# First block's score maps: q and k split in place, and the two maps of a job run on the two halves of the array's rows in turns

## The chip, the core and the metric

The kernel runs on one core of a Trainium2 chip. The metric is the device time of one launch in microseconds. The core has a matrix engine (TensorE, PE in the profile; its weight loads are shown as PEld), a vector engine (DVE), a scalar engine (ACT), GpSimd (POOL), and a sync engine (SP) that issues most DMAs. PE writes its results into PSUM banks; DVE and ACT read them from there.

## The reference, cut to what matters

Two transformer blocks run one after the other on 256 rows of 2048 numbers. The first has two layers; each is a product with `w_in`, a differential attention, two side branches and a product with `w_out`. The change touches the scores of that attention alone. There are 8 heads, and each head has two maps `i` of 64 numbers:

```python
def _diff_attn(qb, k_all, v_all, lam):
    s = jnp.einsum('bqhid,bkhid->bhiqk', qb.astype(jnp.float32) * ATTN_SCALE, k_all.astype(jnp.float32))
    p = jax.nn.softmax(s, axis=-1)
    a = p[:, :, 0] - lam * p[:, :, 1]
    return jnp.einsum('bhqk,bkhe->bqhe', a.astype(v_all.dtype), v_all)
```

In layer 0 the 256 context rows attend to themselves (256 keys) and the 256 rows of x attend to context and x (512 keys). In layer 1 only the rows of x attend (512 keys).

## The kernel before, in words

Every large product is made of three matmuls in the one-pass type `fp32r`: each operand is split into a rounded part (hi) and the rest (lo), and hi·hi, hi·lo and lo·hi are summed in a PSUM bank (`mm3`, L247 to L249; where the two parts of an activation lie side by side, two matmuls do it, L267 and L269). The weights come in blocks of 512 KB by DMA (L177, L182). ACT makes hi of a block (L185) and DVE makes lo (L186).

The attention of the first block is a generator (`attention`) that is stepped beside the weight products: `bg_step` takes one step of it after every chunk of weights (in layer 1 after every second chunk). It works in **jobs**: a job is 128 query rows of one head. Layer 0 has 4 jobs a head, two with 256 keys and two with 512; layer 1 has 2 jobs a head with 512 keys. With 8 heads that makes 48 jobs, 16 with 256 keys and 32 with 512. Attention runs four heads at a time, so there are four groups of jobs in the span.

For each head `parts(h)` prepares the operands. A head's `q` and `k` are tiles of 128 partitions: map 0 lies on partitions 0 to 63 and map 1 on 64 to 127. For each map it builds a stacked `q` (hi in the map's own half, lo in the other half; L649 on ACT, L650 on DVE), a `k` with its hi in both halves (L651 and L652 on ACT), and the lo of `k` in the map's half (L653 on POOL). All of these work on 64 partitions.

For each job `scores` then runs, map after map, two matmuls into one PSUM bank: L663 over all 128 rows (it gives hi·hi and lo·hi at once) and L664 over the 64 rows of the map's half (hi of q times lo of k). DVE takes the row maximum (L665), ACT the exponential (L672), DVE normalises and subtracts (L676 to L679); two steps later PE transposes (L686), and at the end of a head multiplies with v (L696) and transposes again (L712).

The PSUM tiles of the attention (`aux`) come from a ring of three banks. A job takes two of them for its maps, and a third goes to the transposes of an older job. The `qs` tiles come from a ring of ten.

The Python order is not quite the order on the engines. A scheduler of the framework places instructions by its own cost model, within the data dependencies. So it can put weight matmuls between the maps of a job: in 18 of the 48 jobs of before, weight matmuls or transposes stand between the two maps. Each engine then runs its own list in order.

The side work that the rows name: L404 and L406 on DVE are products with the modulation weights, spread over the first half of the span; L416 and L434 sum their result over the partitions with a 32-column operand per stream, in plain fp32 (each is recorded as two passes), and L423 transposes it on 64 rows; L339 and L340 are the helper `split` (hi on ACT, lo on DVE).

## Time and profile before

| what | value |
|---|---|
| median of 3 runs | 2966.14 us (2965.07 to 2972.32) |
| the profiled execution: its own time | 2966.39 us |
| its span | 2964.5 us |
| PE, DVE, ACT, POOL busy, share of the span | 98%, 67%, 41%, 10% |
| granted TensorE clock, mean | 0.991 of 2.4 GHz |

A page of the profile gives busy times over the whole span; rows by stretch give them for a part of it, timeline rows give the start of each instruction and its recorded duration. Matmuls are pipelined, so the duration of one overlaps the next. What a matmul costs the engine is read from the distance between its start and the start of the next one, called pitch here.

### The profile page before, as it was taken

To read this page: it belongs to the slowest core of one execution; us is meant where nothing else is said; L and a number is where in the kernel's file an instruction comes from. 1 tells how busy PE (TensorE), PEld (TensorE's weight loads), DVE (VectorE), ACT (ScalarE), POOL (GpSimd) and SP (SyncE) were. 2 spreads that over 40 slices of the span, in tenths; PEclk is the share of its full clock that TensorE was granted. 3 is DMA by queue.
4 is the path that set the end of the run, shared out by engine and by line. 5 is a ranking of instruction groups with operands and counts; after the bars stand their busy time and mean duration, and the time that the engine had idled before them with its cause. 6 is when DMAs were issued, how large, how long until landed. Compare 5 with 4: busy or idle time off the path is not lost.

```text
span 2964.5 us, 38716 instructions
## 1 busy us (share of the span) xinstructions
PE 2899.2 (98%) x14802; PEld 2382.4 (80%) x14802; DVE 1978.0 (67%) x2890; ACT 1213.7 (41%) x1750; POOL 296.9 (10%) x319
## 2 busy tenths in 40 slices
PE   8999999999999999999988999999999999999998
PEld 5677778678779787878876888888888888888887
DVE  3779987887985649568665565766655556555564
ACT  3123433432311436246434454544444434444444
POOL 0001001101100411011210000000101102011011
PEclk9999999999999999999998999999999999999999
DMA  8764445346664336545754545455565655555555
GB/s 308 265 204 136 130 154 177 128 142 211 215 196 164 121 116 199 166 137 184 243 176 135 185 144 198 157 187 190 185 197 166 195 190 184 199 185 192 191 187 169
DMA packets 156435, 533.86 MB, mean 180 GB/s; under 512 B 17860, under 2 KB 21196, under 8 KB 156248
## 3 DMA queue, kind: packets, MB, share of 16 engines
q1 hardware_dynamic: 148656, 510.79, 52.2%
q0 software_dynamic: 5632, 18.36, 2.0%
q10 hardware_dynamic: 1960, 2.22, 0.3%
q8 instruction: 116, 1.90, 0.3%
q14 instruction: 71, 0.58, 0.1%
HBM read 527.07 MB, written 4.23 MB: 179 GB/s over the span
## 4 chain that ended last, share of the span: by engine, by line
PE 71%; issue 5%; DVE 2%; DMA 1%; ACT 1%; POOL 0%; ACTq 0%; POOLq 0%; DVEq 0%
PE acc L267 22%; PE acc L269 11%; PE acc L247 11%; PE acc L249 11%; PE acc L248 11%; PE aux L696 1%; PE aux L664 1%; PE aux L663 0%; DVE lo L186 0%; PE aux L686 0%; PE aux L1083 0%; ACT hi L185 0%; DVE p L952 0%; DMA raw<-in_w_in_dram 0%; POOL small L123 0%
## 5 line engine op out<-in xcount | busy, mean ns | idle before, releaser
L186 DVE TENSOR_TENSOR lo<-raw,hi 128x1024 fp32r<-128x1024 f32 x766 | 942.1, 1233 | 683.9 <-ACT hi L185 677.9
L185 ACT CAST hi<-raw 128x1024 fp32r<-128x1024 f32 x769 | 805.4, 1050 | 1355.1 <-PE acc L249 472.3
L267 PE MATMUL acc<-act,hi 128*128 128x512 f32 x2960 | 1052.1, 400 | 0.6 <-DVE qs L306 0.6
L269 PE MATMUL acc<-act,lo 128*128 128x256 f32 x2960 | 830.7, 281 | 4.6 <-DVE lo L186 4.6
L267 PEld LDWEIGHTS acc<-act,hi 128*128 128x128 f32 x2960 | 555.3, 188 | 139.8 <-issue 3.5
L247 PE MATMUL acc<-hi,act 128*128 128x512 f32 (+1 forms) x1568 | 582.7, 372 | 1.5 <-ACT act L339 1.3
L248 PE MATMUL acc<-lo,act 128*128 128x512 f32 (+1 forms) x1568 | 578.9, 369 | 0.2 <-DVE lo L186 0.2
L249 PE MATMUL acc<-hi,act 128*128 128x512 f32 (+1 forms) x1568 | 578.4, 369 | 0.5 <-DVE act L340 0.5
L269 PEld LDWEIGHTS acc<-act,lo 128*128 128x128 f32 x2960 | 558.3, 189 | 8.2 <-DVE lo L186 6.3
L406 DVE SCALAR_TENSOR_TENSOR ma<-mod,cc,ma 128x512 f32<-128x512 f32 x480 | 344.1, 756 | 25.2 <-DMA mod<-in_w_mod_dram 23.4
L247 PE MATMUL acc<-act,hi 128*128 128x512 f32 x896 | 359.2, 401 | 0.5 <-DVE p L764 0.5
L249 PE MATMUL acc<-act,lo 128*128 128x512 f32 x896 | 351.7, 393 | 0.0
L248 PE MATMUL acc<-act,hi 128*128 128x512 f32 x896 | 351.6, 392 | 0.0
L247 PEld LDWEIGHTS acc<-hi,act 128*128 128x128 f32 x1568 | 296.4, 189 | 54.4 <-issue 3.2
L248 PEld LDWEIGHTS acc<-lo,act 128*128 128x128 f32 x1568 | 296.7, 189 | 50.1 <-DVE lo L186 1.4
L249 PEld LDWEIGHTS acc<-hi,act 128*128 128x128 f32 x1568 | 296.4, 189 | 49.9 <-DVE act L340 1.1
L247 PEld LDWEIGHTS acc<-act,hi 128*128 128x128 f32 x896 | 168.8, 188 | 55.3 <-issue 9.4
L249 PEld LDWEIGHTS acc<-act,lo 128*128 128x128 f32 x896 | 168.8, 188 | 39.3 <-issue 3.6
L248 PEld LDWEIGHTS acc<-act,hi 128*128 128x128 f32 x896 | 168.9, 189 | 35.6 <-issue 3.0
L315 DVE TENSOR_REDUCE tmp<-acc 128x256 f32<-128x512 f32 x169 | 112.9, 684 | 52.2 <-PE acc L269 52.2
L1190 POOL TENSOR_TENSOR tmp<-tmp 128x256 f32<-128x256 f32 x64 | 69.7, 1089 | 566.8 <-ACT tmp L1189 539.4
L340 DVE TENSOR_TENSOR act<-tmp,act 128x256 fp32r<-128x256 f32 (+1 forms) x96 | 58.3, 614 | 45.7 <-ACT act L339 45.7
(214 smaller groups left out, 1792.5 us busy)
## 6 DMA issues: line engine op xcount, KB each, us to landing
raw<-in_w_in_dram SPq DMA_DIRECT2D x384, 512.0 KB, 3.4
mod<-in_w_mod_dram SPq DMA_DIRECT2D x158, 512.0 KB, 3.9
raw<-in_w_up_dram SPq DMA_DIRECT2D x128, 512.0 KB, 4.4
raw<-in_w_down_dram SPq DMA_DIRECT2D x128, 512.0 KB, 4.3
raw<-in_w_out_dram SPq DMA_DIRECT2D x96, 512.0 KB, 4.3
mod<-in_w_mod_dram SPq DMA_DIRECT2D x68, 256.0 KB, 5.0
raw<-in_w_proj_a_dram SPq DMA_DIRECT2D x16, 512.0 KB, 3.8
raw<-in_w_proj_b_dram SPq DMA_DIRECT2D x16, 512.0 KB, 4.3
```

Source lines behind the costliest of these rows:

```text
L185: S.copy(hi, raw)
L186: (fn or V).tensor_sub(lo, raw, hi)
L247: mm(ps, lh, rh, start=start, stop=False)
L248: mm(ps, lh, rl, start=False, stop=False)
L249: mm(ps, ll, rh, start=False, stop=stop)
L267: mm(p[:w, :].rearrange("p (a t) -> p a t", a=2), hi[:, kk, c:c + w], act.both(k0 + kk, tok), start=start, stop=False)
L269: mm(p[:w, :ntok], lo[:, kk, c:c + w], ah[:, tok], start=False, stop=stop)
L315: V.reduce_sum(t, ps[0], axis=AX.X)
L340: V.tensor_sub(lo, src, h)
L406: V.scalar_tensor_tensor(st[s], raw[:, kk, :], cc2[:, k, s:s + 1], st[s], op0=ALU.mult, op1=ALU.add)
L664: mm(p[:, :nk], qi[r, q0:q0 + P], kl[r, 0:nk], start=False, stop=True)
L1190: G.tensor_mul(t, t, t)
```

## The change

It does four things, all in the attention of the first block:

- `parts` no longer builds stacked copies. It calls the helper `split` on the whole `q` tile and on the whole `k` tile of a head: one ACT cast and one DVE subtraction each, over 128 partitions. It takes 4 `qs` tiles a head where there were 5. POOL has no part in it any more.
- `scores` takes both PSUM banks of a job first.
- Each map's scores are three matmuls over the 64 rows of its own half (hi·hi, hi·lo, lo·hi) where there were one over 128 rows and one over 64. A job has six matmuls where it had four.
- The six are written in turns: map 0 on the lower half of the rows into its bank, map 1 on the upper half into its own, three times.

```diff
         def parts(h):
-            q, k = qt_[h], kt_[h]
-            nq, nk = q.shape[-1], k.shape[-1]
-            r = lambda n: qs_tile()[:, :n].bitcast(F32R)
-            L, H = slice(0, 64), slice(64, P)
-            a0, a1, b0, b1, kl = r(nq), r(nq), r(nk), r(nk), r(nk)
-            for t, b, s, d in ((a0, b0, L, H), (a1, b1, H, L)):
-                S.copy(t[s], q[s])
-                V.tensor_sub(t[d], q[s], t[s])
-                S.copy(b[s], k[s])
-                S.copy(b[d], k[s])
-                G.tensor_sub(kl[s], k[s], b[s])
-            return (a0, b0, kl, L), (a1, b1, kl, H)
+            res = []
+            for t in (qt_[h], kt_[h]):
+                res.append(tuple(qs_tile()[:, :t.shape[-1]].bitcast(F32R) for _ in range(2)))
+                split(res[-1], t)
+            return res

         def scores(h, qk, job):
             q0, o, nk = job
             mx, sums = small(2), small(2)
             ps = []
-            for i in range(2):
-                qi, ki, kl, r = qk[i]
-                p = aux()
-                mm(p[:, :nk], qi[:, q0:q0 + P], ki[:, 0:nk], start=True, stop=False)
-                mm(p[:, :nk], qi[r, q0:q0 + P], kl[r, 0:nk], start=False, stop=True)
+            (qh, ql), (kh, kl) = qk
+            ps = [aux(), aux()]
+            for n, (a, b) in enumerate(((qh, kh), (qh, kl), (ql, kh))):
+                for i, p in enumerate(ps):
+                    r = slice(64 * i, 64 * i + 64)
+                    mm(p[:, :nk], a[r, q0:q0 + P], b[r, 0:nk], start=n == 0, stop=n == 2)
+            for i, p in enumerate(ps):
                 V.reduce_max(mx[:, i:i + 1], p[:, :nk], axis=AX.X)
-                ps.append(p)
```

From here on a line below the diff stands six lines earlier than before (L658 is the new matmul of the scores; L665 becomes L660, L672 becomes L666).

The scheduler places the new matmuls too. The second job of the first head (256 keys) stands on PE like this before; the number behind `aux` tells the bank's tile, so the map:

```order
L249 MATMUL acc_2344<-act_129,lo_2229 128x512
L663 MATMUL aux_2385<-qs_2262,qs_2260 128x256
L664 MATMUL aux_2385<-qs_2264,qs_2260 128x256
L663 MATMUL aux_2389<-qs_2263,qs_2261 128x256
L664 MATMUL aux_2389<-qs_2264,qs_2261 128x256
L247 MATMUL acc_2341<-act_129,hi_2279 128x512
```

The same place after:

```order
L249 MATMUL acc_2339<-act_129,lo_2229 128x512
L658 MATMUL aux_2380<-qs_2264,qs_2260 128x256
L658 MATMUL aux_2381<-qs_2264,qs_2260 128x256
L658 MATMUL aux_2380<-qs_2265,qs_2260 128x256
L658 MATMUL aux_2381<-qs_2265,qs_2260 128x256
L658 MATMUL aux_2380<-qs_2264,qs_2261 128x256
L658 MATMUL aux_2381<-qs_2264,qs_2261 128x256
L247 MATMUL acc_2336<-act_129,hi_2272 128x512
```

Here the six stand in turns, as written. So they do in 37 of the 48 jobs (24 with 512 keys, 13 with 256). In 3 jobs (two with 512 keys, one with 256) the order is map 0, 0, 1, 1, 0, 1. In the other 8 the scheduler took the maps apart. The fourth job of the first head (512 keys) is one of these, on PE after:

```order
L248 MATMUL acc_2489<-act_126,hi_2406 128x512
L658 MATMUL aux_2530<-qs_2264,qs_2260 128x512
L658 MATMUL aux_2530<-qs_2265,qs_2260 128x512
L658 MATMUL aux_2530<-qs_2264,qs_2261 128x512
L249 MATMUL acc_2489<-act_126,lo_2407 128x512
L247 MATMUL acc_2489<-act_126,hi_2406 128x512
L248 MATMUL acc_2489<-act_126,hi_2406 128x512
L249 MATMUL acc_2489<-act_126,lo_2407 128x512
L658 MATMUL aux_2531<-qs_2264,qs_2260 128x512
L658 MATMUL aux_2531<-qs_2265,qs_2260 128x512
L658 MATMUL aux_2531<-qs_2264,qs_2261 128x512
```

The three matmuls of a map stand together there, with weight matmuls between the maps; of the 8 such jobs 6 have 512 keys and 2 have 256. On ACT the first head's preparation reads before:

```order
L649 CAST qs_2260<-p32_422 64x512
L651 CAST qs_2262<-p32_349 64x512
L652 CAST qs_2262<-p32_349 64x512
L649 CAST qs_2261<-p32_422 64x512
L651 CAST qs_2263<-p32_349 64x512
L652 CAST qs_2263<-p32_349 64x512
```

and after:

```order
L185 CAST hi_2228<-raw_2226 128x1024
L339 CAST qs_2260<-p32_422 128x512
L430 DMA tmp_2442<-in_b_mod_dram 64x512
L339 CAST qs_2264<-p32_349 128x512
L185 CAST hi_2272<-raw_2270 128x1024
```

Six casts became two. The order of everything else is nearly what it was on each engine.

## Rows read from the trace of the kernel before

**Rows 1.** The page: span and two engines, busy us, share, instructions.

```profile
span 2964.5 us, 38716 instructions
PE 2899.2 (98%) x14802; PEld 2382.4 (80%) x14802; DVE 1978.0 (67%) x2890; ACT 1213.7 (41%) x1750; POOL 296.9 (10%) x319
```

**Rows 2.** The page: the chain that ended last, by engine.

```profile
PE 71%; issue 5%; DVE 2%; DMA 1%; ACT 1%; POOL 0%; ACTq 0%; POOLq 0%; DVEq 0%
```

**Rows 3.** Two job stretches: length, busy PE, PEld, DVE, ACT, POOL, clock, DMA.

```profile
270.00:410.00 140.00, 137.95 (x620) 103.05 (x620) 129.89 (x238) 64.33 (x128) 16.25 (x12) 1.00 0.40 130
...
1110.00:1185.00 75.00, 72.69 (x398) 57.80 (x397) 72.73 (x119) 47.83 (x83) 12.25 (x8) 1.00 0.59 193
```

**Rows 4.** PE's waits from 270 to 1400: us, times, longest.

```profile
PE acc L269 <- DVE lo L186: 4.6, 4, 1.3
PE aux L663 <- ACT pp L672: 4.6, 3, 3.1
```

**Rows 5.** Timeline of PE, a job with 512 keys: start, us, instruction.

```profile
1124.72 0.40 PE L663 MATMUL aux<-qs 128*128 128x512 f32 x1
...
1126.32 0.50 PE L267 MATMUL acc<-act,hi 128*128 128x512 f32 x1
1126.65 0.28 PE L269 MATMUL acc<-act,lo 128*128 128x256 f32 x1
1126.77 0.40 PE L267 MATMUL acc<-act,hi 128*128 128x512 f32 x1
```

**Rows 6.** Timeline of PE, a job with 256 keys.

```profile
277.76 0.39 PE L248 MATMUL acc<-act,hi 128*128 128x512 f32 x1
277.99 0.39 PE L249 MATMUL acc<-act,lo 128*128 128x512 f32 x1
278.21 0.28 PE L663 MATMUL aux<-qs 128*128 128x256 f32 x1
...
279.36 0.50 PE L247 MATMUL acc<-act,hi 128*128 128x512 f32 x1
279.70 0.40 PE L248 MATMUL acc<-act,hi 128*128 128x512 f32 x1
```

**Rows 7.** PE, the matmuls of 32 columns: by form, then a timeline row.

```profile
L434 PE MATMUL aux<-ma,ones 128*32 128x512 f32 x24 | 8.4, 605 | 0.0
...
293.97 1.05 PE L434 MATMUL aux<-ma,ones 128*32 128x512 f32 x4
```

**Rows 8.** Timeline of PE, a run of four matmuls on 64 rows.

```profile
520.16 0.46 PE L423 MATMUL aux<-ident,ma 64*128 64x64 f32 x4
```

**Rows 9.** Timeline of PE and its weight loads behind a job.

```profile
296.66 0.50 PE L247 MATMUL acc<-act,hi 128*128 128x512 f32 x1
296.77 0.19 PEld L248 LDWEIGHTS acc<-act,hi 128*128 128x128 f32 x1
```

**Rows 10.** By form: what prepares the operands (busy us, mean ns), and `split`.

```profile
L653 POOL TENSOR_TENSOR qs<-p,qs 64x512 fp32r<-64x512 f32 x32 | 46.3, 1448 | 141.6 <-ACT qs L651 126.1 <-PE acc L269 15.0
L652 ACT CAST qs<-p 64x512 fp32r<-64x512 f32 x32 | 19.8, 619 | 0.8
L339 ACT CAST act<-p 128x512 fp32r<-128x512 f32 x16 | 8.8, 618 | 0.0
L340 DVE TENSOR_TENSOR act<-p,act 128x512 fp32r<-128x512 f32 x16 | 10.1, 682 | 0.0
```

**Rows 11.** Timeline of DVE: one kind of instruction beside L653 on POOL, and not.

```profile
517.63 1.79 DVE L406 SCALAR_TENSOR_TENSOR ma<-mod,cc,ma 128x512 f32<-128x512 f32 x1
...
526.83 0.74 DVE L406 SCALAR_TENSOR_TENSOR ma<-mod,cc,ma 128x512 f32<-128x512 f32 x1
```

**Rows 12.** PE's longest wait for a bank, and the stretch behind it.

```profile
538.12 0.58 PE L663 MATMUL aux<-qs 128*128 128x256 f32 x1 [3.08 <-ACT pp L672]
...
537.40:544.20 6.80, 6.08 (x14) 4.58 (x15) 6.80 (x15) 1.02 (x4) 0.00 (x0) 0.50 0.64 220
544.20:551.00 6.80, 6.80 (x28) 4.79 (x28) 4.32 (x10) 2.34 (x6) 0.00 (x0) 1.00 0.34 110
```

## The prediction

> **What bounds the kernel now.** I read the page's engines and chain first, then the stretches with attention jobs, then what PE waits for in them, then single jobs in PE's timeline. PE is busy for 98% of the span [rows 1], and the chain that ended last is 71% PE with 5% "issue" and hardly anything else [rows 2]. In two of the four stretches that hold the jobs PE is busy 137.95 of 140 us and 72.69 of 75, at the full clock [rows 3]. So a microsecond of PE's stream that goes there should leave the span, unless DVE takes over: it is busy 129.89 of the 140 and 72.73 of the 75 [rows 3]. PE's waits that belong here are small: 4.6 us for DVE's lo of a weight block, in 4 pieces, and 4.6 us for a PSUM bank that ACT still reads, 3.1 of them in one piece [rows 4].

> **What a job costs PE now.** All pitches are start to start. A plain matmul of 512 columns has a pitch of 0.23 us [rows 6], one of 256 columns 0.12 [rows 5]. A job with 512 keys takes 1.60 us from its first L663 to the next weight matmul, and that one has a pitch of 0.33 instead of 0.23 [rows 5]: 1.70 us in all. Four plain matmuls would take 0.92, so 0.78 goes elsewhere. A job with 256 keys takes 1.15 plus 0.34 − 0.23 = 0.11 [rows 6], so 1.26, less 4 × 0.12 = 0.48: again 0.78. The same rest at both widths says that it goes by events and not by columns. The events are the four changes between 128 and 64 rows in a job, 0.195 us each.

> **What a job costs after.** A run of 64-row matmuls now has two changes of row count, in and out: 0.39 us. That changes count, and not the matmuls of a run, is also what four matmuls of 64 rows in one run show: 0.46 us together [rows 8].

> The open price is the alternation: whether a matmul on rows 0 to 63 and one on rows 64 to 127 run side by side. No row of before has two such neighbours. The nearest are matmuls that use different columns of the array: four records of L434, 605 ns each, 2.4 us if laid end to end, take 1.05 us together [rows 7]. So parts of the array do work side by side on this chip. The other end is six matmuls in a row at the plain pitch. I take side by side, because rows 7 are the only rows with parts of the array in use. Then a job in turns has three slots instead of six:

> - 512 keys: 0.39 + 3 × 0.23 = 1.08, a gain of 0.62. 256 keys: 0.39 + 3 × 0.12 = 0.75, a gain of 0.51.
> - Order 0, 0, 1, 1, 0, 1: four slots, 1.31 and 0.87, a gain of 0.39 either way.
> - Maps taken apart: two runs, so four changes, and six slots: 0.78 + 1.38 = 2.16, a loss of 0.46; with 256 keys 0.78 + 0.72 = 1.50, a loss of 0.24.

> By the order on PE these are 24 and 13, 2 and 1, 6 and 2 jobs: 14.9 + 6.6 + 0.8 + 0.4 − 2.8 − 0.5 = **19.4 us gained**.

> A weight load goes with every matmul, so a pair has two, and with 256 keys they might not fit into 0.12 us. If loads of 128 columns share one path at 0.12 each, a pair takes 0.24 and the 256-key jobs in turns gain 0.15 instead of 0.51: 4.7 us less. The four loads beside L423 came in 0.46 us with their matmuls [rows 8], about 0.12 each at most, which leaves this open; it is in the range.

> [...] I give that 0.05 of the 0.72 below.

> **The other engines.** ACT's six casts a head, 0.62 us each, become two of 0.62 [rows 10]; nothing waits long for them, so I cost that at nothing. DVE keeps two subtractions a head, 0.68 us on 128 partitions [rows 10], and hands out lo of k itself where POOL did: the count stays, since it no longer makes one for each half of q. POOL loses 32 instructions of 1.45 us [rows 10]. That is not its own time that matters, but DVE's: an L406 that runs beside L653 takes 1.79 us, one without 0.74 [rows 11]. If each of the 32 held up DVE by up to 1.05 us, DVE gets up to 34 us back, some 8 in each of the four groups, while PE needs it 5 us earlier in each. So DVE doesn't become the bound; it may even shorten the 4.6 us that PE waits for lo. I take 2 us of these.

> Against that stands a new wait. PE now needs both banks before it can pass on: the second matmul of a job waits for the bank that the older exponential still reads, and all weight matmuls queue behind it on PE. Before, the scheduler had put other work between the maps in 18 jobs; now in 8. Ten jobs lose that filler. The price in the one bad place of before is 3.08 us, after which the clock stood at 1.2 instead of 2.4 GHz for 6.8 us, with 14 matmuls where the next 6.8 us had 28 [rows 12]: 3.4 us more. That place may get better (DVE was held up by POOL just ahead of it) or worse; minus 6.5 to plus 7, and I take plus 2. These two terms cancel.

> The profiled execution took 2966.39 us, 1.9 more than its span and within 0.3 of the median of 2966.14, so no correction is needed: 2966.4 − 19.4 = **2947**.

> **The rivals.**

> *The halves run one after the other* (the change doesn't do what it says). A job in turns, or 0, 0, 1, 1, 0, 1, then has six slots and two changes: 0.39 + 1.38 = 1.77, a loss of 0.07 in 26 jobs; 0.39 + 0.72 = 1.11, a gain of 0.15 in 14. With the 3.3 us lost in the jobs taken apart: 3.0 us lost, **2969**. For it: no row shows two row halves at once, and both halves write all 128 partitions of PSUM, which the four records of L434 do not. Against it: rows 7. [...] Chance 0.13.

> *Each change of half costs what a change of row count costs* (slower). The place is inside the run: five inner changes in a job in turns, three in the other order. A change costs 0.195: with 512 keys 7 × 0.195 + 1.38 = 2.75, a loss of 1.05 in 24 jobs; with 256 keys 1.37 + 0.72 = 2.09, a loss of 0.83 in 13; the three others lose 1.8, the eight 3.3. Sum 41 us, **3007**. It decides from about 0.03 us a change on: 37 × 5 + 9 = 194 inner changes on top of the 3.0 us. For it: every change of row count costs so now. Against it: the pairs of L434 change columns and pay nothing like it [rows 7]. Chance 0.08.

> *The gain goes into the bank wait.* If two more jobs stall PE for 3 us and halve the clock behind them, 13 us are gone: **2960**. For it: the ten jobs without filler. Against it: of the three bank waits of before only one reached 3 us [rows 4], and ACT and DVE have less queued now. Chance 0.07.

> **How the numbers follow.** Side by side 0.72: 2947, alone 2936 (stall and half clock of rows 12 gone, all of the wait for lo gone) to 2957 (loads one after another, filler missed). One after the other 0.13 at 2966 to 2974, bank wait 0.07 at 2957 to 2963, change of half 0.08 at 3000 and more. The range 2935 to 2972 leaves out the last and a little at each end. About 0.3% is what a measurement of this kernel can tell from no change, so faster means under 2957.2: 0.69 of the first case and 0.02 of the third; slower means over 2975: 0.08 and 0.01 of the second; the rest, 0.20, is no change.

> **What the profile after would show.** Right: in a job in turns the six L658 start in three pairs, a few ns within a pair, 0.23 us (0.12 with 256 keys) from pair to pair, and the job takes about 1.1 us from the first L658 to the next weight matmul; L653 is gone from POOL, and no L406 near a job takes 1.8 us. One after the other: six starts 0.23 us apart, about 1.8 us. A change of half that costs: starts 0.42 us apart. A bank wait: an idle time of PE ahead of the second L658 of a job, put down to the exponential, with a stretch of clock 0.50 behind it. What would make me wrong with the mechanism right is the price of loads in 256-key jobs, and waits that the scheduler no longer covers.

## The result and the profile after

The changed kernel takes **2932.6 us** in the median (2930.1 to 2934.8, 4 runs), against 2966.5 for the kernel before. The ratio is 0.988, interval 0.987 to 0.989. A second set of runs gave 2932.6 again and 0.989 (0.987 to 0.990). The forecast was faster, 2947, with a range down to 2935. So the direction was right, the gain of 34 us was 1.75 times the 19.4 forecast, and the time lies 2.4 us below the range.

The page after (engines, then the chain; columns as in [rows 1] and [rows 2]):

```profile
span 2928.3 us, 38793 instructions
PE 2871.4 (98%) x14898; PEld 2371.6 (81%) x14898; DVE 1946.9 (66%) x2890; ACT 1179.6 (40%) x1688; POOL 249.3 (9%) x287
PE 72%; issue 5%; DVE 3%; DMA 1%; ACT 1%; POOL 1%; POOLq 0%; ACTq 0%; DVEq 0%
```

PE is still the bound: 98% of a shorter span, with 96 matmuls more. The two stretches of [rows 3] read now (length, busy PE, PEld, DVE, ACT, POOL, clock, DMA):

```profile
270.00:410.00 140.00, 139.82 (x690) 106.94 (x689) 127.11 (x246) 59.99 (x120) 4.39 (x3) 1.00 0.42 139
1110.00:1185.00 75.00, 74.60 (x434) 61.77 (x433) 60.95 (x112) 37.46 (x64) 4.08 (x4) 1.00 0.50 166
```

PE is idle for 0.2 us of the first instead of 2.1, and 0.4 of the second instead of 2.3. DVE fell from 72.73 to 60.95 in the second, POOL from 16.25 to 4.39 in the first. (The same clock times hold a little more of the program now.)

A job with 256 keys and one with 512, both in turns, in PE's timeline after (start, us, instruction; equal neighbours are merged):

```profile
277.66 0.39 PE L249 MATMUL acc<-act,lo 128*128 128x512 f32 x1
277.98 0.62 PE L658 MATMUL aux<-qs 64*128 64x256 f32 x6
278.53 0.50 PE L247 MATMUL acc<-act,hi 128*128 128x512 f32 x1
...
329.57 0.39 PE L249 MATMUL acc<-act,lo 128*128 128x512 f32 x1
329.89 0.96 PE L658 MATMUL aux<-qs 64*128 64x512 f32 x6
330.78 0.51 PE L247 MATMUL acc<-act,hi 128*128 128x512 f32 x1
331.12 0.38 PE L680 MATMUL aux<-ident,pp 128*128 128x128 f32 x2
```

From the first L658 to the next weight matmul it is 0.55 us with 256 keys ([rows 6]: 1.15) and 0.89 with 512 ([rows 5]: 1.60). Add 0.10 us, by which the run starts later than the plain pitch behind the matmul ahead of it, and 0.11 for the longer pitch of the matmul behind it: 0.76 and 1.10, where the forecast had 0.75 and 1.08. Inside the run the six starts come in pairs 3 to 4 ns apart; the second pair follows the first by 0.33 us with 512 keys and 0.22 with 256 (0.10 more than the plain pitch, as behind a change of row count in [rows 5]), the third by 0.23 and 0.11. So the halves do run side by side, and the loads of two 256-column matmuls fit into one slot of 0.11 us.

Not every run pairs up like this. The two stretched by a run of L423 aside, 34 do and four do not. In those four the semaphores show that the bank of the second map came free after the run had begun, and its first load started some 43 ns later. Three of them are the jobs with the order 0, 0, 1, 1, 0, 1. One, on PE and with its weight loads:

```profile
585.11 0.93 PE L658 MATMUL aux<-qs 64*128 64x256 f32 x6
585.11 0.72 PEld L658 LDWEIGHTS aux<-qs 64*128 64x128 f32 x6 [0.24 <-ACT pp L666]
```

It takes 0.93 us where a paired run takes 0.62. So a part of the bank wait doesn't show as idle time of PE: the matmuls of the first map go on alone.

PE's waits in the part of the span that holds the first block's attention (270 to 1360 us):

```profile
PE aux L913 <- ACT p L906: 5.9, 1, 5.9
PE aux L658 <- ACT pp L666: 1.2, 1, 1.2
PE aux L680 <- DVE tmp L700: 1.1, 4, 0.4
PE aux L913 <- DVE tmp L916: 0.8, 1, 0.8
PE acc L249 <- DVE act L340: 0.5, 1, 0.5
```

Of [rows 4], the 4.6 us for lo of a weight block are gone, and the 4.6 us for a bank are 1.2. The place of [rows 12] has changed too. The first line is PE's wait there, the other two show its clock ahead of and behind it:

```profile
526.43 0.62 PE L658 MATMUL aux<-qs 64*128 64x256 f32 x5 [1.19 <-ACT pp L666]
...
520.00:526.40 6.40, 5.25 (x23) 3.92 (x21) 6.40 (x12) 0.58 (x3) 0.00 (x0) 1.00 0.49 177
526.40:533.20 6.80, 6.77 (x31) 5.32 (x32) 6.80 (x15) 1.99 (x4) 0.00 (x0) 1.00 0.70 230
```

PE waits 1.19 us instead of 3.08, and the granted clock stays at 1.00: 31 matmuls behind it in 6.8 us, where the kernel before had 14 at 0.50.

Where did 36 us of span go? For every run of score matmuls I took the time from the start of the matmul ahead to that of the second one behind, less the plain pitches of those two neighbours and less the waits that the trace shows. Summed over all jobs this is **78.7 us before and 56.1 after: 22.6 us**. PE's other idle time from 260 to 1400 us went from 18.5 to 10.4: **8 us**. The half clock of [rows 12] is gone: **3.4 us**. That is 34, less about 1 us that is counted twice, because one job of the kernel before ran at half clock. Another 1.7 us is a stretch of half clock of 3.4 us near the start, which is missing in this profile; it is there again in the profile of the same kernel as e5, so it is not a gain of the change. The rest is small change.

### The profile page after: what moved, and what is told of

It reads as the page before. It is cut to its first block, busy times and chain, and to the rows that moved or that the text cites. A ratio compares the mean times of both kernels' runs of the same rounds, so it can differ in the third digit from the quotient of the medians.

```text
span 2928.3 us, 38793 instructions
## 1 busy us (share of the span) xinstructions
PE 2871.4 (98%) x14898; PEld 2371.6 (81%) x14898; DVE 1946.9 (66%) x2890; ACT 1179.6 (40%) x1688; POOL 249.3 (9%) x287
## 4 chain that ended last, share of the span: by engine, by line
PE 72%; issue 5%; DVE 3%; DMA 1%; ACT 1%; POOL 1%; POOLq 0%; ACTq 0%; DVEq 0%
PE acc L267 23%; PE acc L247 11%; PE acc L269 11%; PE acc L249 11%; PE acc L248 11%; PE aux L658 1%; PE aux L690 1%; DVE lo L186 1%; DVE ma L406 1%; PE aux L680 0%; POOL small L123 0%; PE aux L1077 0%; ACT hi L185 0%; DMA raw<-in_w_in_dram 0%; DVE small L660 0%
## 5 line engine op out<-in xcount | busy, mean ns | idle before, releaser
L406 DVE SCALAR_TENSOR_TENSOR ma<-mod,cc,ma 128x512 f32<-128x512 f32 x480 | 339.1, 744 | 28.1 <-DMA mod<-in_w_mod_dram 26.7
```

Of the source, the lines that this page charges most:

```text
L406: V.scalar_tensor_tensor(st[s], raw[:, kk, :], cc2[:, k, s:s + 1], st[s], op0=ALU.mult, op1=ALU.add)
```

## The experiments

All ratios are to the kernel before, run beside each on the same chip; it took 2967 to 2968 us each time.

### POOL makes the lo of k again

```diff
-                split(res[-1], t)
+            split(res[0], qt_[h])
+            (kh, kl), k = res[1], kt_[h]
+            S.copy(kh, k)
+            for s in (slice(0, 64), slice(64, P)):
+                G.tensor_sub(kl[s], k[s], kh[s])
```

> The changed kernel (2932.6 us), but the lo of k comes from POOL again, two subtractions on 64 partitions a head as before; casts, matmuls and their order of turns stay. Theory P (POOL held DVE up, and that made PE wait): 2941 to 2945 us; L406 takes 1.8 us again beside the subtractions, and PE waits again for lo of weights and for the exponential, 5 to 9 us in all. Rival A (it was ACT's fewer casts) and rival S (it was the scheduler's new order alone): 2931 to 2935, PE's waits as in the changed kernel.

Measured: 2956.9 us, ratio 0.996 (0.994 to 0.997). Of the gain of 34 us 11 are left; theory P had expected a smaller loss (2941 to 2945). The score matmuls nearly keep their price (58.6 us by the sum above). PE's waits are back (from 260 to 1400 us):

```profile
PE aux L662 <- ACT pp L670: 8.2, 4, 4.7
PE aux L684 <- ACT pp L670: 2.8, 2, 1.6
PE aux L684 <- DVE tmp L436: 2.3, 1, 2.3
PE aux L684 <- DVE p L711: 2.2, 2, 1.3
```

The first is a bank that the exponential still reads, the others results that ACT or DVE give to the transposes. Three stretches of half clock stand behind such waits, 20 us together, at 303, 539 and 1126 us. PE's idle time from 260 to 1400 us is 24.5 us, where the changed kernel has 10.4. As expected, an L406 takes up to 1.78 us again, where the longest in the changed kernel takes 0.76. The expectation named the waits for lo of weights too; those did not come back. Rivals A and S fall.

### Six casts on ACT

```diff
+                for s in (slice(0, 64), slice(64, P)):
+                    S.copy(res[-1][1][s], t[s])
                 split(res[-1], t)
```

> The changed kernel, with four more casts on ACT for each head (64 partitions each, written to the tiles of lo before lo is made), so six as before. Theory P: the waits of PE stay as in the changed kernel; the scheduler takes the maps of 11 or 12 jobs apart instead of 8, worth about 4 us, so 2934 to 2939. Rival A: the waits come back too, 2942 to 2947. Rival S: order changes and waits with it, anything from 2930 to 2945.

Measured: 2937.0 us, ratio 0.990 (0.988 to 0.991), so some 4 us above the changed kernel. The score matmuls cost 58.6 instead of 56.1, which is what theory P expected from more jobs taken apart. PE's wait for a bank is 1.5 us instead of 1.2, and here 3.4 us of half clock follow it, 1.7 us lost:

```profile
530.34 0.62 PE L660 MATMUL aux<-qs 64*128 64x256 f32 x3 [1.48 <-ACT pp L668]
...
532.30:535.70 3.40, 3.40 (x10) 2.66 (x9) 3.40 (x9) 0.00 (x0) 0.00 (x0) 0.50 0.61 201
```

So ACT's lighter load is worth some 2 us at most in itself.

### Map after map

```diff
-            for n, (a, b) in enumerate(((qh, kh), (qh, kl), (ql, kh))):
-                for i, p in enumerate(ps):
-                    r = slice(64 * i, 64 * i + 64)
+            for i, p in enumerate(ps):
+                r = slice(64 * i, 64 * i + 64)
+                for n, (a, b) in enumerate(((qh, kh), (qh, kl), (ql, kh))):
                     mm(p[:, :nk], a[r, q0:q0 + P], b[r, 0:nk], start=n == 0, stop=n == 2)
```

> The changed kernel, but a job's six matmuls are written map after map (three on the lower half of the rows, then three on the upper) instead of in turns. Side by side: only the last of map 0 and the first of map 1 can pair, five slots instead of three, so 27 jobs lose 0.46 us and 14 lose 0.24, less what jobs not in turns lost already: about 15 us, 2945 to 2949. If the turns are worth nothing and the gain came from elsewhere: 2931 to 2935.

Measured: 2934.4 us, ratio 0.989 (0.987 to 0.990). Neither reason that I had written down holds. The turns are indeed worth nothing that can be measured, but the gain did not come from elsewhere. The same job as above, in this kernel's timeline of PE:

```profile
331.16 0.39 PE L249 MATMUL acc<-act,lo 128*128 128x512 f32 x1
331.48 0.96 PE L658 MATMUL aux<-qs 64*128 64x512 f32 x6
332.38 0.51 PE L247 MATMUL acc<-act,hi 128*128 128x512 f32 x1
```

It is 0.96 us again, and the six starts again come as three pairs, now 10 ns apart instead of 3. The program has all three matmuls of map 0 ahead of those of map 1, in 27 jobs with 512 and 14 with 256 keys. In 36 of these 41 the trace has three pairs. A record doesn't tell its map, but in the next experiment, where all six stand on one half, two starts with 512 keys are 0.22 us apart at least. So I read the pairs as the first of map 1 beside the first of map 0. In the other five the first matmul of map 1 starts only when ACT or DVE lets go of its bank. The score matmuls cost 56.6 us. So what counts here is that the two halves' matmuls stand in one run and that both banks are free when it begins, not their order.

### Both maps on the lower half

```diff
-                    r = slice(64 * i, 64 * i + 64)
+                    r = slice(0, 64)
```

> The changed kernel, but both maps are computed on the lower half of the rows (map 0 twice, so the second map of the reference is left out), each still into its own bank. All else stays. If the halves side by side carry the job sum: six slots in a run, 26 jobs with 512 keys lose 3 x 0.23 us and 14 with 256 keys 3 x 0.12, about 23 us, so 2953 to 2960, with starts 0.23 us apart. If the fewer changes of row count carry it: 2932 to 2937.

This kernel leaves the second map out and computes the first one twice. Measured: 2951.4 us, ratio 0.994 (0.993 to 0.996): 19 us of the gain are gone. The same job, timeline of PE:

```profile
333.87 0.39 PE L249 MATMUL acc<-act,lo 128*128 128x512 f32 x1
334.19 1.66 PE L658 MATMUL aux<-qs 64*128 64x512 f32 x6
335.78 0.50 PE L247 MATMUL acc<-act,hi 128*128 128x512 f32 x1
```

1.59 us to the next weight matmul, 0.89 in the changed kernel: three slots of 0.23 more. The score matmuls cost 78.0 us, as before the change (78.7). So all that PE saves on the scores is the two halves side by side; fewer changes of row count only pay for the two matmuls more.

### The kernel before, lo of k on DVE

```diff
-                G.tensor_sub(kl[s], k[s], b[s])
+            S.copy(kl, k)
+            V.tensor_sub(kl, k, kl)
             return (a0, b0, kl, L), (a1, b1, kl, H)
```

> The kernel before (2966.5 us) with its stacked operands and four matmuls a job; only the lo of k is made by DVE on 128 partitions, after one more cast on ACT, and POOL has none of it. Theory P: half of what the job sum left unexplained or more, 2954 to 2959 us, PE's waits for lo and for the exponential mostly gone. Rival A: 2966 or a little above, since ACT has one more cast. Rival S: 2962 to 2970, with no L406 of 1.8 us and yet the waits.

Measured: 2954.8 us, ratio 0.996 (0.994 to 0.997): **13 us gained without touching one matmul**, and with more work for DVE and ACT. The score matmuls cost 78.2 us, as before. PE's waits from 270 to 1400 us, to be held against [rows 4]:

```profile
PE aux L664 <- ACT pp L673: 1.8, 3, 1.3
```

No wait for lo of a weight block is left, and no half clock between 17 and 972 us. PE's idle time from 260 to 1400 us is 9.1 us instead of 18.5, and with the 3.4 us of [rows 12] that is the 13.

### POOL works for nobody

The changed kernel; DVE makes both lo, and POOL makes that of k as well, in 64 small pieces, into a tile that is never read.

```diff
+    idle = cst.tile([P, 256], F32, name="idle")
...
+            for s in (slice(0, 64), slice(64, P)):
+                for c in (slice(0, 256), slice(256, 512)):
+                    G.tensor_sub(idle[s, :], kt_[h][s, c], res[1][0][s, c])
             return res
```

> The changed kernel, with DVE making both lo as it does; POOL makes the lo of k as well, in pieces of 64 partitions by 256 columns, into a tile that nobody reads. If POOL's mere activity holds DVE up: the loss of e1 comes back, at least half of its 24 us, so 2943 to 2960, with PE waiting for the exponential. If e1 was slow because its score matmuls waited for POOL's late result: 2932 to 2937.

Measured: 2949.7 us, ratio 0.994 (0.993 to 0.995). Against the changed kernel beside it (2932.6) that is 17 us lost to work that no instruction needs. PE, ACT and DVE have the same instructions in the same order as in the changed kernel, so the scheduler's order is no rival here. PE's idle time from 260 to 1400 us is 20.6 us where the changed kernel has 10.4: it waits 6.7 us for banks (1.2 there) and 6.2 for what the transposes read (1.1). 5.0 us of the first are in one piece, at the place of [rows 12]:

```profile
533.48 1.01 PE L662 MATMUL aux<-qs 64*128 64x256 f32 x5 [4.98 <-ACT pp L670]
...
533.50:540.30 6.80, 6.80 (x21) 5.37 (x22) 6.80 (x15) 1.32 (x3) 0.00 (x0) 0.58 0.73 232
```

How POOL gets there is read on DVE. At that place the exponential waits for the row maxima, which stand in DVE's list behind four L406. They start 7.4 us after the job's first matmul in the kernel before, 3.7 after the change and 6.9 here. DVE is not busy all that time: the four L406 wait for a transfer of modulation weights. The kernel before, then the changed kernel, then this one, first the transfer's issue:

```profile
527.60 0.33 SPq L177 DMA_DIRECT2D mod<-in_w_mod_dram  x1
530.88 2.74 DVE L406 SCALAR_TENSOR_TENSOR ma<-mod,cc,ma 128x512 f32<-128x512 f32 x4 [0.72 <-DMA mod<-in_w_mod_dram]
...
515.30 0.33 SPq L177 DMA_DIRECT2D mod<-in_w_mod_dram  x1
519.64 2.74 DVE L406 SCALAR_TENSOR_TENSOR ma<-mod,cc,ma 128x512 f32<-128x512 f32 x4 [1.30 <-DMA mod<-in_w_mod_dram]
...
522.45 0.33 SPq L177 DMA_DIRECT2D mod<-in_w_mod_dram  x1
526.17 2.74 DVE L406 SCALAR_TENSOR_TENSOR ma<-mod,cc,ma 128x512 f32<-128x512 f32 x4 [0.69 <-DMA mod<-in_w_mod_dram]
```

The transfer is issued when an earlier L406 has given its buffer back; in the kernel before the sync engine waits 9.5 us for that. That is 1.5 us after the job's first matmul in the kernel before, 3.3 us ahead of it after the change and 0.6 us after it here. So I read the chain as: POOL holds DVE up (22 us over its groups, below), DVE gives a buffer back late, the next weights come late, and row maxima, exponential and bank follow.

DVE's groups by form from 260 to 1400 us (busy us, mean ns), first the changed kernel (e5), then this one:

```profile
L340 DVE TENSOR_TENSOR qs<-p,qs 128x512 fp32r<-128x512 f32 x24 | 16.3, 686 | 0.0
L662 DVE TENSOR_SCALAR small<-small 128x2 f32<-128x2 f32 x48 | 7.7, 160 | 0.0
L660 DVE TENSOR_REDUCE small<-aux 128x1 f32<-128x512 f32 x64 | 42.4, 683 | 1.3 <-PE aux L658 1.1
```

```profile
L340 DVE TENSOR_TENSOR qs<-p,qs 128x512 fp32r<-128x512 f32 x24 | 20.1, 844 | 0.0
L666 DVE TENSOR_SCALAR small<-small 128x2 f32<-128x2 f32 x48 | 12.1, 252 | 0.0
L664 DVE TENSOR_REDUCE small<-aux 128x1 f32<-128x512 f32 x64 | 42.3, 681 | 0.9 <-PE aux L662 0.8
```

The subtraction for the `qs` tiles (686 to 844 ns) and the small scalar products (160 to 252) got slower, the row maxima, which read PSUM, did not (683 and 681). Over all of DVE's groups in that stretch the change of the means, times their counts, is 22 us. By what POOL's work holds these instructions up no run shows.

A part of the loss is left open: these pieces also hold their `qs` tiles longer, and e1 lost 23 to 24 us where this kernel lost 17, with POOL's result needed there and not here.

### A fourth bank

```diff
-    ps_mm = pool("psmm", 5, space=PSUM)
-    ps_ax = pool("psax", 3, space=PSUM)
+    ps_mm = pool("psmm", 4, space=PSUM)
+    ps_ax = pool("psax", 4, space=PSUM)
```

> The changed kernel with four PSUM banks for the attention instead of three, and four instead of five for the weight products. The scheduler leaves 46 of 48 jobs in one run instead of 40. If what is left to gain is in the jobs taken apart: six jobs less with a second run at about 1 us each, 2926 to 2929. If the weight products need their fifth bank: each product's first matmuls wait for the last read of the one before, 2940 or more.

Measured: 2944.8 us, ratio 0.992 (0.991 to 0.993), 12 us worse than the changed kernel. Both halves of the expectation came true: the score matmuls cost only 48.6 us, and the products pay more than that, most of it in the second block. From 1500 us on PE now waits at the start of a product, which it does not do in the changed kernel (by form, busy us, mean ns, idle before and what ended it):

```profile
L267 PE MATMUL acc<-act,hi 128*128 128x512 f32 x2304 | 818.6, 400 | 8.1 <-DVE tmp L315 7.3 <-DVE act L1003 0.4
```

Next I let one bank change hands: the attention has it in the first block, the products from the second block on.

```diff
...
+    def bank(kind, p, bufs, name):
+        taken[kind] += 1
+        if lent[0] == kind and taken[kind] % (bufs + 1) == 0:
+            return ps_x.tile([P, 512], F32, tag="x", name=name)
+        return p.tile([P, 512], F32, tag=kind, name=name)
...
+    lent[0] = "mm"
```

> The changed kernel with one PSUM bank that changes hands: the attention of the first block has four and the weight products four, from the second block on it is three and five as before. If e8 lost its time in the second block's products alone: the gain of e8 before 1400 us stays, 3 to 7 us, and nothing is lost behind: 2925 to 2930. If four banks cost the products of the first block as well: 2932 or more.

Measured: 2937.0 us, ratio 0.990 (0.988 to 0.991). The score matmuls cost 53.6 us, so 2.6 less than in the changed kernel, but the time is 4 us worse. Most of that arises between 1405 and 1435 us, behind the last job, where layer 1's last product runs with its four banks and 3.4 us of half clock appear. With the rotation's cosine product moved from POOL to DVE on top:

```diff
-            G.tensor_mul(m, t, csc("rc"))
+            V.tensor_mul(m, t, csc("rc"))
```

> e9, with the cosine product of the rotation on DVE instead of POOL (28 instructions of 0.93 us beside the attention). If POOL's activity still costs PE something there: 1 to 4 us less than e9. If PE no longer waits on DVE there: the same as e9 within 1 us, or a little more, since DVE has 12 us more to do.

Measured: 2938.4 us, ratio 0.990 (0.989 to 0.992): no gain. None of these beats the changed kernel.

### The changed kernel again

No edit: it gives the level for the three kernels run beside it (e6, e7 and e8).

> The changed kernel once more, as the measure for the other runs of this call: 2932 to 2936 us.

Measured: 2932.6 us, ratio 0.989 (0.987 to 0.990), with the score matmuls at 56.2 us.

### Two parts, four kernels

| | POOL makes lo of k | DVE makes it |
|---|---|---|
| four matmuls, stacked | 1 (the kernel before) | 0.996: 13 us gained |
| six matmuls, two halves | 0.996: 11 us gained | 0.988: 34 us gained |

The two parts are worth 24 us apart and 34 together. With POOL at work the halves bring only half of their 22 us: PE then reaches the bank before DVE and ACT have freed it, and waits (24.5 us idle in e1, 18.5 in the kernel before, and 20 us at half clock where that has 7).

## Why the prediction was right and wrong

**The bound and the mechanism: right.** PE's stream was the bound, and time taken out of it left the span. In a paired run the first matmuls of the two halves start 3 to 4 ns apart, the change of row count costs about 0.2 us each time, twice in a run (0.76 less three slots of 0.12) as it did four times before (0.78), and the loads of 256-column pairs fit (0.11 us from the second pair to the third). All three rivals fall: halves one after the other (e7 is that case, and it lies 19 us higher), a price on each change of half (none is seen; the pitch inside the run is the plain one, 0.23 and 0.11 us), and the bank wait (1.2 us, and four runs that don't pair up).

**Weight loads.** The 0.05 of the 0.72 was for loads that wait until the matmul on their own half has ended; no run shows such a wait. In the job with 512 keys above, the loads of the third pair start at 330.225 and 330.228 us, just behind the matmuls of the second (330.222 and 330.226, 0.39 us each), and the third pair follows at the plain pitch of 0.23 us (0.11 with 256 keys). So in these jobs the loads for a half overlap the running matmul of that half, as in [rows 9], where a load for all rows starts 0.11 us into a matmul of 0.50.

**The job sum: 19.4 forecast, 22.6 measured.** The price after was right (55.1 by the forecast's prices for its 48 jobs, 56.1 measured). The price before was too low: 1.70 and 1.26 us times their counts make 74.6, and the trace has 78.7. I had read two jobs that lie between plain weight matmuls. Others paid more: about 0.87 us a run of two in the jobs taken apart with 512 keys, so 1.75, about 2.1 behind the 32-column matmuls, and one job ran at half clock. A sum over all 48 would have shown it.

**The step that failed: "These two terms cancel."** I took 2 us for POOL's part and gave 2 us back for a longer bank wait. Measured, POOL's part is worth 13 us by itself (e4), and the bank wait shrank from 4.6 to 1.2 us. The prediction had the mechanism ([rows 11], up to 34 us of DVE's time), wrote that it "may even shorten" the 4.6 us for lo, and noted that DVE was held up just ahead of the bad bank wait. But it set the ten jobs without filler against that, by a guess, and no row gave either figure. What it didn't follow is how the bank hangs on DVE: buffer, weights, row maxima, exponential, free bank. So both of PE's waits had one cause, and it went away. The two terms were not independent and did not point in opposite directions. All the good ends came together: lo gone (4.6), bank wait down (3.4), half clock gone (3.4), which are the 11 us of the range's lower end. That end, 2936, was right for these terms; the 3.2 us of the job sum then carried the time out of the range.

**The order on PE.** I priced 24 and 13 jobs by their being written in turns. That was right in number and wrong in reason: e3 has no job in turns and gets nearly the same price. The three jobs with the order 0, 0, 1, 1, 0, 1 took about 1.1 us (256 keys) and 1.5 (512), where the forecast had 0.87 and 1.31 for four slots; the trace shows a bank that came free late in each. Beside the four runs with a late bank, only the eight jobs with weight matmuls between the maps lose the pairing. One map of such a job alone takes as long as both maps of another (changed kernel):

```profile
300.33 0.96 PE L658 MATMUL aux<-qs 64*128 64x512 f32 x3
```

**ACT's casts: right** within 2 us (e2), the scheduler's order aside.

## What to carry to other kernels

Matmuls that use half of the rows are worth pairing with the other half: here two maps cost one (six matmuls with 512 columns took 0.96 us, six on one half 1.66), as long as both stood in one run, in either order, and both banks were free when it began. When a change takes work off GpSimd (worth 13 us here without touching one matmul), look for what DVE does meanwhile, and follow DVE's lateness to everything that waits for it, transfers into its buffers too, before calling two effects independent. And price a sum over all instances, not over two clean ones.
